# Turning the attention's value rows by VectorE blocks and a DRAM round trip in place of TensorE transposes

## The chip, the core and the metric

The kernel runs on one core of one Trainium2 chip. The metric is the device time of one execution in microseconds (us), as the median of several runs; lower is better. Engines are named as in the profile: PE is TensorE's matmul, PEld its weight load, DVE is VectorE, ACT is ScalarE, POOL is GpSimd, SP is SyncE, which here only issues DMAs. A name with q (SPq, DVEq) is an engine's instruction queue.

## What is computed

One step of a hybrid decoder layer: a prompt of 512 tokens and 8 samples of 4 tokens, model width 1024. The part that matters here is the sliding-window attention of the prompt:

```python
h = RMSNorm_pre(x)
x_r, q, k, v, g = split(h @ W_in)            # q: 8 heads of 128, k and v: 2 heads of 128
# per block of 128 queries: keys and values of this block and of the one before
s = q @ k.T * 128**-0.5 + rel_bias           # masked to the band
p = softmax(s with a learned sink per head)
o = p @ v                                    # (128 queries) x (128 columns of the head)
p_win_v = v[-128:]                           # the last 128 value rows are also an output
```

Beside it run an RG-LRU branch, an attention of the samples against a cache, gated output projections, and a convolutional feed-forward part.

## The kernel before

Activations are held turned, as columns by tokens: a projection tile is 128 columns (on partitions) by 512 prompt tokens and 32 sample tokens. Every float32 product is made of three fp32r matmuls: an operand X is split into a rounded part XH (ScalarE copy, L283, L710) and the rest XL (VectorE subtract, L168, L290), and the product is XH·WH, XL·WH and XH·WL, all by `mm` (L165).

The program is written as a list of *steps*. One step is one 128-column group of `W_in` on one half of the tokens (24 matmuls into a tile `pmin`), and behind each step stands a *tick*. A tick runs side jobs that are Python generators: each `yield` ends the job's turn, and `yield 3` skips two ticks. The order in which side jobs place their instructions between the steps is so the order on PE, DVE, ACT and POOL, which keep program order there. SP's order is made by the framework's scheduler. An engine works strictly in order, so an instruction that waits holds up all behind it.

The steps of this stage follow the list `qkv_order`: key 0, value 0, query heads 0 to 3, key 1, value 1, query heads 4 to 7. Side jobs between them:

- `attn_unit(hp, n)`, 16 of them: scores of two heads for query block n (tile `psc`, 6 matmuls), scaling and bias (`s`, DVE L177), softmax with exponentials on ACT (L781) and small DVE steps around them (`st`), a block transpose on DVE (`pb`, L823), its store to DRAM (`pd`, L826) and four loads back (`pt`, L831), the split of `pt` into `tH` (ACT, L834) and `tL` (DVE), and the product with the values (tile `pvp`: vH·tH, vL·tH, vH·tL). So the probabilities already go the way that the change gives to the values.
- `v_tok(kv, v)`, once for each of the two value heads: it turns the value tile `v` (head columns by tokens) to tokens by columns, which `pvp` needs as weights, splits it into `vH` and `vL`, and writes the last 128 rows to the output through `vout`.
- `sample_attn(g)`: the attention of the samples; its softmax ends at the DVE line L789 on tile `ss`, and PE turns the result at L911 (`pst`).
- weight splits (`wh_in`, `wl_in`) and weight loads (`raw_in`, 512 KB each, on SP), two weights ahead of their use.

Temporary tiles such as `v`, `s`, `tH` and `tL` come from one pool of 10 buffers (`T`), auxiliary PSUM tiles such as `pv`, `psc` and `pvp` from a pool of 5 (`PX`).

Of the kernel before, what the change touches and what calls it, by code (L numbers as in the profile page):

```python
# [11 lines left out]
F32 = mybir.dt.float32  # L12
F32R = mybir.dt.float32r
AF = mybir.ActivationFunctionType
# [3 lines left out]
P = 128  # L18
# [105 lines left out]
def hawk_step(ctx, tc, I, O):  # L124
    nc = tc.nc
    act, dve, pool, pe = nc.scalar, nc.vector, nc.gpsimd, nc.tensor
# [9 lines left out]
    drp = ctx.enter_context(tc.tile_pool(name="scratch", bufs=1, space=bass.MemoryType.DRAM))  # L136
# [9 lines left out]
    def T(name, dt=F32):  # L146
        return tp.tile([P, FLAT + 4], dt, tag="t", name=name)
# [7 lines left out]
    def PX(name):  # L155
        return psx.tile([P, 512], F32, tag="aux", name=name)

    def SM(name, shape, tag="sm"):
        return smp.tile(shape, F32, tag=tag, name=name)

    def f32(ap):
        return ap.bitcast(F32)
# [4 lines left out]
    def sub(out, a, b):  # L167
        dve.tensor_tensor(out=out, in0=a, in1=b, op=ALU.subtract)  # L168
# [51 lines left out]
    ident = keep.tile([P, P], F32, name="ident")  # L220
# [181 lines left out]
    pv = keep.tile([P, 96], F32, name="pv")  # L402
# [303 lines left out]
    Q, K, V, A = Full("q"), Full("k"), Full("v"), Full("a")  # L706
# [39 lines left out]
    vtmp = {}  # L746

    def v_tok(kv, v):
        px = PX(f"pv{kv}")
        for n in range(4):  # L750
            pe.transpose(px[:, n * P:(n + 1) * P], v[:, n * P:(n + 1) * P], ident)
        yield
        vh, vl = V.alloc(kv)
        act.activation(vh[:, 0:512], px, AF.Copy)
        sub(vl[:, 0:512], px, f32(vh[:, 0:512]))
        vo = SM(f"vout{kv}", [P, P])
        dve.tensor_copy(vo, px[:, 384:512])
        pool.dma_start(out=O["p_win_v"][0, 0, :, kv, :], in_=vo)
        yield

    def v_done(kv, a, ps):
        lo, hi = HALF[a]
        if a == 0:
            vtmp[kv] = T(f"v{kv}")
        v = vtmp[kv]
        scaled(v[:, lo:hi], ps, a)
        if a == 1:
            act.copy(vn[:, kv, :], v[:, SEQ:NT])
            start_at(now[0] + 1, v_tok(kv, v))
# [1030 lines left out]
    for i, x in enumerate(plan):  # L1800
# [8 lines left out]
        else:  # L1809
            _, q, c, a = x  # L1810
# [198 lines left out]
    v, r, s_, b_, h_ = (st[:, z:z + 1] for z in range(5))  # L2009
# [52 lines left out]
```

## Time and profile before

| what | value |
|---|---|
| median of 3 runs | 972.03 us (971.7 to 972.34) |
| the profiled execution | 972.46 us |
| its span, first to last instruction | 970.7 us |
| PE busy | 960.7 us, 99% |
| DVE busy | 761.6 us, 78% |
| ACT busy | 550.5 us, 57% |
| POOL busy | 167.9 us, 17% |
| mean granted TensorE clock | 0.999 of full speed (2.4 GHz) |
| DMA | 152 GB/s mean over the span |

All times of day below are in us from the start of the span. The profiled execution lasted 1.76 us longer than its span, and 0.43 us longer than the median run. A busy share is a mean over stages; what a change in one stage is worth is read from that stage's waits.

### The profile page before, as it was taken

Reading aid. Unit: us, or ns where it says so; the run is one execution under the profiler, and the core shown is the slowest. Engines: PE = TensorE matmul, PEld = TensorE weight load, DVE = VectorE, ACT = ScalarE, POOL = GpSimd, SP = SyncE. Lnnn points to the kernel's source line nnn. Section 1 sums busy time; section 2 is a strip of 40 time slices with the busy share of each in tenths; the row PEclk is TensorE's granted clock in tenths of the full one; section 3 lists DMA queues with packets and bytes.
Section 4 is the critical chain, followed back from the end, with each engine's and each line's share of the span. In section 5 each row is a group of like instructions: output and inputs, shape, how many; then the busy total and the mean of one; then the engine's idle time right before and its main releaser. Section 6 shows DMA issues by size and latency. Waiting matters only on the chain.

```text
span 970.7 us, 20070 instructions
## 1 busy us (share of the span) xinstructions
PE 960.7 (99%) x7598; PEld 952.3 (98%) x7598; DVE 761.6 (78%) x1623; ACT 550.5 (57%) x1342; POOL 167.9 (17%) x282
## 2 busy tenths in 40 slices
PE   9999999999999999999999999999999999999997
PEld 8999999999999999999999999999999999999996
DVE  5778888857858555599967878787888888888886
ACT  6544533467476425566867665555555565656642
POOL 2152000003406231230011110101011111111024
PEclk9999999999999999999999999999999999999999
DMA  7865435532334537236147576767667675858632
GB/s 222 239 216 182 146 92 146 154 106 88 96 99 152 177 107 187 64 106 195 46 108 196 133 182 147 183 153 175 162 160 189 151 192 136 205 132 232 185 136 92
DMA packets 248412, 147.26 MB, mean 152 GB/s; under 512 B 37332, under 2 KB 232796, under 8 KB 248284
## 3 DMA queue, kind: packets, MB, share of 16 engines
q1 hardware_dynamic: 237324, 124.15, 43.4%
q0 software_dynamic: 9696, 19.42, 11.7%
q10 hardware_dynamic: 1296, 2.43, 0.7%
q8 instruction: 59, 0.97, 0.4%
q14 instruction: 37, 0.30, 0.1%
HBM read 118.21 MB, written 16.74 MB: 139 GB/s over the span
## 4 chain that ended last, share of the span: by engine, by line
PE 89%; DVE 6%; ACT 2%; issue 1%; DMA 1%; POOL 0%; DVEq 0%; ACTq 0%; SPq 0%; POOLq 0%
PE pmin L165 20%; PE pux L1529 16%; PE pmdn L165 16%; PE puy L1529 8%; PE pq L1529 6%; PE pmlo L165 5%; PE pmao L165 5%; PE pmout L165 4%; PE puz L1529 4%; PE pg L165 1%; PE pvp L165 1%; PE psc L165 1%; DVE ft L174 0%; DVE wl_e L168 0%; DVE wl_dl L168 0%
## 5 line engine op out<-in xcount | busy, mean ns | idle before, releaser
L165 PE MATMUL pmin<-hH,wh_in 128*128 128x256 f32 (+1 forms) x568 | 163.9, 291 | 0.0
L165 PE MATMUL pmin<-hL,wh_in 128*128 128x256 f32 (+1 forms) x568 | 162.4, 288 | 0.0
L165 PE MATMUL pmin<-hH,wl_in 128*128 128x256 f32 (+1 forms) x568 | 159.1, 288 | 0.0
L165 PE MATMUL pmdn<-fH,wh_dn 128*128 128x256 f32 (+1 forms) x448 | 129.2, 288 | 0.0
L165 PE MATMUL pmdn<-fH,wl_dn 128*128 128x256 f32 (+1 forms) x448 | 129.0, 288 | 0.0
L165 PE MATMUL pmdn<-fL,wh_dn 128*128 128x256 f32 (+1 forms) x448 | 128.9, 288 | 0.0
L165 PEld LDWEIGHTS pmin<-hH,wh_in 128*128 128x128 f32 x568 | 107.2, 189 | 1.2 <-issue 1.0
L165 PEld LDWEIGHTS pmin<-hL,wh_in 128*128 128x128 f32 x568 | 107.2, 189 | 0.1
L165 PEld LDWEIGHTS pmin<-hH,wl_in 128*128 128x128 f32 x568 | 104.7, 188 | 0.2 <-issue 0.2
L177 DVE SCALAR_TENSOR_TENSOR uc<-u,fv,uc 128x560 f32<-128x560 f32 x128 | 102.0, 797 | 1.7 <-ACT uc L1560 1.1
L165 PEld LDWEIGHTS pmdn<-fH,wl_dn 128*128 128x128 f32 x448 | 84.4, 188 | 0.0
L165 PEld LDWEIGHTS pmdn<-fL,wh_dn 128*128 128x128 f32 x448 | 84.3, 188 | 0.1
L165 PEld LDWEIGHTS pmdn<-fH,wh_dn 128*128 128x128 f32 x448 | 84.3, 188 | 0.1
L1657 ACT COPY u<-pux 128x272 f32<-128x272 f32 x52 | 20.1, 387 | 86.5 <-PE pux L1529 86.5
L168 DVE TENSOR_TENSOR u<-puy,u 128x240 f32<-128x240 f32 (+2 forms) x78 | 24.6, 344 | 47.8 <-PE puy L1529 30.7
L174 DVE TENSOR_TENSOR ft<-ft,pmdn 128x256 f32<-128x256 f32 (+1 forms) x104 | 45.1, 434 | 16.4 <-PE pmdn L165 16.4
L283 ACT ACTIVATE wh_in<-raw_in 128x512 fp32r<-128x512 f32 x70 | 42.2, 625 | 19.0 <-issue 10.6
L290 DVE TENSOR_TENSOR wl_in<-raw_in,wh_in 128x512 fp32r<-128x512 f32 x70 | 47.8, 693 | 1.0 <-ACT wh_in L283 1.0
L1560 ACT ACTIVATE uc<-u,fv 128x560 f32<-128x560 f32 x64 | 48.2, 755 | 0.0
L781 ACT ACTIVATE s<-s,st 128x256 f32<-128x256 f32 (+1 forms) x32 | 15.2, 475 | 53.0 <-DVE st L778 45.3
L168 DVE TENSOR_TENSOR wl_dn<-raw_dn,wh_dn 128x512 fp32r<-128x512 f32 x56 | 38.3, 684 | 3.6 <-ACT wh_dn L1478 3.6
L1467 POOL DMA_DIRECT2D raw_up_s<-raw_up_s x26 | 22.4, 862 | 93.5 <-DMA raw_up_s<-raw_up__11280 5.4
(744 smaller groups left out, 3371.1 us busy)
## 6 DMA issues: line engine op xcount, KB each, us to landing
raw_in<-in_w_in_dram SPq DMA_DIRECT2D x35, 512.0 KB
raw_dn<-in_w_down_dram SPq DMA_DIRECT2D x56, 256.0 KB
raw_up_s<-in_w_up_dram SPq DMA_DIRECT2D x25, 512.0 KB
raw_up_s<-raw_up_s POOLq DMA_DIRECT2D x26, 256.0 KB, 4.2
raw_ao<-in_w_attn_o_dram SPq DMA_DIRECT2D x8, 512.0 KB
raw_lo<-in_w_lru_o_dram SPq DMA_DIRECT2D x8, 512.0 KB
raw_out<-in_w_out_dram SPq DMA_DIRECT2D x8, 512.0 KB
pd<-pb SPq DMA_DIRECT2D x12, 256.0 KB
```

The lines of the kernel that those rows point to most:

```text
L165: pe.matmul(out, l, r, start=start, stop=stop)
L168: dve.tensor_tensor(out=out, in0=a, in1=b, op=ALU.subtract)
L174: dve.tensor_tensor(out=out, in0=a, in1=b, op=ALU.add)
L177: dve.scalar_tensor_tensor(out=out, in0=a, scalar=s_, in1=b, op0=op0, op1=op1)
L283: act.activation(hl[0], raw, AF.Copy)
L290: (eng or dve).tensor_tensor(out=hl[1], in0=raw, in1=f32(hl[0]), op=ALU.subtract)
L781: act.activation(s3[:, j, :], s3[:, j, :], AF.Exp, bias=ng[:, j:j + 1], accum_out=sm[:, j:j + 1])
L1467: pool.dma_start(out=w["p4"], in_=w["p2"], accum_op=ALU.add)
L1529: pe.matmul(ps[:, :HN], w, x, start=start and k == 0 and i == 0, stop=stop and k == 3 and i == 2, skip_group_check=True)
L1560: act.activation(yt[j][:, 0:FLATU], u[:, 0:FLATU], AF.Copy, scale=fv[:, j:j + 1])
L1657: act.copy(e[nm_], z)
```

## The change

`v_tok` no longer uses PE. DVE turns the 16 32x32 blocks of each 128x128 piece in one instruction (`vb`), SP stores the result to DRAM (`vrows`), four SP loads bring it back with the blocks in their new places, into the tile `v` itself, and the split into `vH` and `vL` reads `v` in SBUF where it read PSUM. The copy for the output goes from DVE to ACT. The job now has three turns behind the first: the loads one tick later, the split three ticks after these, the output copy one tick after that.

```diff
     def v_tok(kv, v):
-        px = PX(f"pv{kv}")
-        for n in range(4):
-            pe.transpose(px[:, n * P:(n + 1) * P], v[:, n * P:(n + 1) * P], ident)
-        yield
-        vh, vl = V.alloc(kv)
-        act.activation(vh[:, 0:512], px, AF.Copy)
-        sub(vl[:, 0:512], px, f32(vh[:, 0:512]))
+        vb = T(f"vb{kv}")[:, 0:512]
+        dve.transpose(vb.rearrange("p (b n d) -> p n b d", b=4, n=4),
+                      v[:, 0:512].rearrange("p (n b q) -> p n b q", n=4, b=4))
+        rows = drp.tile([P, 512], F32, name=f"vrows{kv}")
+        nc.sync.dma_start(out=rows, in_=vb)
+        yield
+        src = rows.rearrange("(a q) (b x) -> b q a x", a=4, b=4)
+        for b in range(4):
+            nc.sync.dma_start(out=v[32 * b:32 * b + 32, 0:512].rearrange("p (a x) -> p a x", a=4), in_=src[b])
+        yield 3
+        vh, vl = (x[:, 0:512].rearrange("p (n a d) -> p n a d", n=4, a=4) for x in V.alloc(kv))
+        vt = v[:, 0:512].rearrange("p (a n d) -> p n a d", a=4, n=4)
+        act.activation(vh, vt, AF.Copy)
+        sub(vl, vt, f32(vh))
+        yield
         vo = SM(f"vout{kv}", [P, P])
-        dve.tensor_copy(vo, px[:, 384:512])
+        act.copy(vo.rearrange("p (a d) -> p a d", a=4), vt[:, 3])
         pool.dma_start(out=O["p_win_v"][0, 0, :, kv, :], in_=vo)
         yield
```

Lines behind this one move by 8 (L823 becomes L831, and so on). On PE the two groups of four transposes are gone and nothing else moves. On the other engines only the rows of `v_tok` move, and a few DMAs of SP beside them.

On SP this stands before, behind the loads of the weights for query heads 6 and 7 (`ohs` and `mk` are tables of the sample attention, `st_b` holds the recurrent states, `pd_0` and `pt_0` belong to attention unit 0):

```order
L259 DMA raw_in_1183<-in_w_in_dram 128x8x128
L669 DMA ohs<-in_c_ohs_dram 128x320
L826 DMA pd_0_831<-pb_0_829 128x256
L673 DMA mk_894<-in_c_msk_dram 128x320
L831 DMA pt_0_898<-pd_0_831 32x4x64 x4
L602 DMA st_b<-strow 32x8x32 x2
L826 DMA pd_1_973<-pb_1_971 128x512
```

And this stands there now:

```order
L753 DMA vrows_743<-vb_741 128x512
L259 DMA raw_in_1186<-in_w_in_dram 128x8x128
L757 DMA v_407<-vrows_743 32x4x128 x4
L834 DMA pd_0_827<-pb_0_825 128x256
L669 DMA ohs<-in_c_ohs_dram 128x320
L673 DMA mk_890<-in_c_msk_dram 128x320
L839 DMA pt_0_894<-pd_0_827 32x4x64 x4
L834 DMA pd_1_969<-pb_1_967 128x512
```

The store of value head 0 now stands ahead of a weight load and its four loads ahead of unit 0's store and the sample tables.

On DVE this stands before, between the softmax of attention unit 2 (`st_2`) and the key of head 1 (`ks_0`, `kL`):

```order
L168 TENSOR_TENSOR st_2_977<-sinkb,st_2_977 128x2
L290 TENSOR_TENSOR wl_in_942<-raw_in_668,wh_in_941 128x512
L171 TENSOR_TENSOR ks_0_1014<-pmin_0_914,rep 128x256
L174 TENSOR_TENSOR st_2_977<-st_2_977 128x2
L787 RECIPROCAL st_2_977<-st_2_977 128x2
L789 TENSOR_SCALAR s_2_975<-s_2_975,st_2_977 128x256 x2
```

And this now:

```order
L168 TENSOR_TENSOR st_2_973<-sinkb,st_2_973 128x2
L168 TENSOR_TENSOR vL_982<-v_407,vH_981 128x512
L290 TENSOR_TENSOR wl_in_938<-raw_in_668,wh_in_937 128x512
L171 TENSOR_TENSOR ks_0_1014<-pmin_0_910,rep 128x256
L174 TENSOR_TENSOR st_2_973<-st_2_973 128x2
L795 RECIPROCAL st_2_973<-st_2_973 128x2
```

`vL` of value head 0, which stood some 20 rows earlier, is now the first row behind the small softmax steps, ahead of the two rows that DVE did while ACT made the exponentials.

On ACT this stands before at the same place (`tH_0` is the split of unit 0's probabilities):

```order
L782 ACTIVATE st_2_977<-st_2_977 128x2
L283 ACTIVATE wh_in_1011<-raw_in_668 128x512
L710 ACTIVATE kH_1016<-ks_0_1014 128x256
L283 ACTIVATE wh_in_1071<-raw_in_714 128x512
L834 ACTIVATE tH_0_1083<-pt_0_898 128x256
```

And this now:

```order
L790 ACTIVATE st_2_973<-st_2_973 128x2
L761 ACTIVATE vH_981<-v_407 128x512
L283 ACTIVATE wh_in_1011<-raw_in_668 128x512
L765 COPY vout_1041<-v_407 128x128
L710 ACTIVATE kH_1016<-ks_0_1014 128x256
L283 ACTIVATE wh_in_1074<-raw_in_714 128x512
L842 ACTIVATE tH_0_1086<-pt_0_894 128x256
```

`vH` now stands behind the exponentials of unit 2, and `vout` is a row of ACT. For value head 1 the same rows stand later: `vb` behind the copy `kout` of key 1, `vL` behind unit 2 of the second head pair, `vout` behind the exponentials of its unit 3.

## Rows read from the trace of the kernel before

**Rows 1.** The page's part 1: busy us (share of the span) xinstructions, by engine.

```profile
PE 960.7 (99%) x7598; PEld 952.3 (98%) x7598; DVE 761.6 (78%) x1623; ACT 550.5 (57%) x1342; POOL 167.9 (17%) x282
```

**Rows 2.** Waits of PE, whole span: who waited for whom, us, times, longest.

```profile
PE ps_warm L165 <- POOL ones L219: 1.0, 1, 1.0
...
PE pst L911 <- DVE ss L789: 0.7, 1, 0.7
```

**Rows 3.** Stages: us, then each engine's busy us (xinstructions), clock, DMA share, GB/s.

```profile
160.00:170.00 10.00, 9.32 (x76) 9.12 (x74) 9.28 (x27) 4.42 (x17) 0.00 (x0) 1.00 0.45 107
```

**Rows 4.** Timeline of PEld, first group of transposes: start, us, engine, line, op, tiles.

```profile
41.88 0.47 PEld L751 LDWEIGHTS pv<-ident,v 128*128 128x128 f32 x4
42.32 0.19 PEld L165 LDWEIGHTS pmin<-hH,wh_in 128*128 128x128 f32 x1
```

**Rows 5.** Timeline of DVE, 40 to 54 us; in brackets idle before, and releaser.

```profile
40.96 1.29 DVE L290 TENSOR_TENSOR wl_in<-raw_in,wh_in 128x512 fp32r<-128x512 f32 x2
43.72 0.46 DVE L168 TENSOR_TENSOR qL<-pmin,qH 128x288 fp32r<-128x288 f32 x1 [1.47 <-ACT qs L712]
...
45.65 0.68 DVE L168 TENSOR_TENSOR vL<-pv,vH 128x512 fp32r<-128x512 f32 x1
46.25 0.28 DVE L757 COPY vout<-pv 128x128 f32<-128x128 f32 x1
...
53.06 0.46 DVE L168 TENSOR_TENSOR qL<-pmin,qH 128x288 fp32r<-128x288 f32 x1 [0.91 <-ACT qs L712]
53.43 0.70 DVE L823 STREAM_TRANSPOSE pb<-s 128x512 f32<-128x512 f32 x1
```

**Rows 6.** Timeline of SP: stores of probabilities and the loads behind them.

```profile
54.16 0.35 SPq L826 DMA_DIRECT2D pd<-pb  x1
...
56.23 2.02 SPq L831 DMA_DIRECT2D pt<-pd  x4
...
61.70 0.34 SPq L826 DMA_DIRECT2D pd<-pb  x1
68.22 1.77 SPq L831 DMA_DIRECT2D pt<-pd  x4
```

**Rows 7.** The chain that ended last, in order of time, 147 to 170 us.

```profile
147.87 4.37 DMA pt<-pd
...
168.87 0.40 DVE ss L789
...
169.41 0.30 PE pst L911
```

**Rows 8.** Timeline of ACT: end of unit 2's exponentials, and the second `vH`.

```profile
56.92 0.19 ACT L782 ACTIVATE st<-st 128x2 f32<-128x2 f32 x1
...
80.19 0.57 ACT L754 ACTIVATE vH<-pv 128x512 fp32r<-128x512 f32 x1
```

**Rows 9.** Timeline of DVE, 55 to 62 us.

```profile
55.87 0.68 DVE L290 TENSOR_TENSOR wl_in<-raw_in,wh_in 128x512 fp32r<-128x512 f32 x1
...
57.14 0.16 DVE L174 TENSOR_TENSOR st<-st 128x2 f32<-128x2 f32 x1 [0.26 <-ACT st L782]
...
59.30 0.46 DVE L171 TENSOR_TENSOR ks<-pmin,rep 128x288 f32<-128x288 f32 x1 [0.20 <-PE pmin L165]
```

**Rows 10.** Timeline of DVE at the second value head.

```profile
80.80 0.69 DVE L168 TENSOR_TENSOR vL<-pv,vH 128x512 fp32r<-128x512 f32 x1 [1.74 <-ACT vH L754]
...
81.61 0.68 DVE L290 TENSOR_TENSOR wl_in<-raw_in,wh_in 128x512 fp32r<-128x512 f32 x1
```

**Rows 11.** Timeline of DVE, 99 to 147 us.

```profile
99.86 0.68 DVE L168 TENSOR_TENSOR tL<-pt,tH 128x512 fp32r<-128x512 f32 x1
...
139.83 0.52 DVE L171 TENSOR_TENSOR xr<-pmin,rep 128x256 f32<-128x256 f32 x2 [0.19 <-PE pmin L165]
...
146.57 0.46 DVE L171 TENSOR_TENSOR ga<-pmin,rep 128x288 f32<-128x288 f32 x1 [1.85 <-PE pmin L165]
```

**Rows 12.** Timeline of PE: the first `tL` product of unit 1, second head pair.

```profile
103.79 0.28 PE L165 MATMUL pvp<-tL,vH 128*128 128x256 f32 x1
```

## The prediction

> **What bounds the kernel now.** I read the page's part 1 first: PE is busy for 960.7 of the 970.7 us of the span [rows 1], so what PE no longer does should come off the end. Then the waits of PE: five groups in the whole span, none above 1.0 us [rows 2]. One of them matters here. At the first turning of the sample attention's probabilities, PE waits 0.7 us for DVE (`pst` for `ss`). The stage view shows why: from 160 to 170 us DVE is busy 9.28 of 10 us while PE is at 9.32 [rows 3]. The chain that ended last says the same: ahead of `pst` at 169.41 it runs through DVE rows, not PE [rows 7]. So from the first key to that place two chains run side by side, PE's and the softmax's loop of DVE and ACT; at 169.4 us the loop ends last, by 0.7 us, and from there on PE leads again. Both must be followed.
>
> **What PE loses.** Two groups of four transposes go. From the first weight load of the first group to the load behind the group are 42.32 - 41.88 = 0.44 us [rows 4], 0.11 for each transpose; the second group, at 74.8, is alike. PE is never idle there, so without the eight it comes to 169 us earlier by 0.88 us, 0.09% of the time. The Trainium skill (VectorE: DVE Perf Modes, section The three transpose paths) gives 390 ns for a 128x128 transpose on TensorE in bf16; by that figure the eight would be 3.1 us, an estimate. The trace has the float32 ones here at 0.11 us, and that is used.
>
> **What DVE and ACT gain in work, value head 0.**
> - `vb`: one turning of 128x512. The same operation on the same shape (`pb`) takes 0.70 us; of `vL`, 0.68 long, the row behind it hides 0.08 [45.65 to 46.25, rows 5], so I take 0.6. It stands where two weight splits began at 40.96, and behind these DVE stood idle for 1.47 us [rows 5]: hidden. If that cover were gone it would be 0.6 us of DVE's loop.
> - The old `vL` and `vout` go from 45.65, some 0.6 + 0.2 us. This too is worth little: at 53.06 DVE waits again, for ACT's rounding of a product of PE [rows 5], so from there it is ahead by PE's 0.44 us and no more.
> - The new `vH` and `vL` stand behind unit 2's exponentials. These end at 56.92 + 0.19 = 57.11 [rows 8], 0.44 earlier now: 56.67. `vH` reads SBUF instead of PSUM; nearest is the old one, 0.57 [rows 8]. It ends at 57.15, since it begins some 0.1 before the row ahead ends. `vL` waits for it: before, DVE spent this time on a weight split and `ks` (55.87 to about 56.9) and so stood still for 0.26 only [rows 9]. Now these come behind `vL`: 57.15 + 0.6 + 0.6 + 0.4 = 58.75 for the row that stood at 57.14. That is 1.6 later; 0.2 to 0.3 is caught at once, since `ks` of the second half stood 0.20 waiting for PE [rows 9]. DVE's loop is late by 1.3 us.
> - `vout` on ACT: 0.2 us (of DVE's 0.28, rows 5, less overlap) ahead of a key split that waits for DVE anyway. Nothing.
>
> **Value head 1.** `vb` has no cover here and adds 0.6: 1.9 late. At 80.80 DVE waited 1.74 us for `vH`, and `vL` and `vout` then took until 81.61 [rows 10]. Gone from that place, they give back 0.8: 1.1 late. The new `vH` is hidden behind a rounding for which DVE waits first, `vL` adds 0.6: 1.7. `vout`, behind exponentials on ACT and ahead of a weight rounding, adds 0.2 to what DVE waits for next: 1.9 us late in absolute time at about 98 us, 1.9 + 0.88 = 2.8 us late against PE.
>
> **Where this lateness goes.** The idle stretches of DVE between 98 and 139 us end on ACT, which had itself waited for DVE; they move with the loop and absorb nothing. Two end on PE's product: 0.19 us at 139.83 and 1.85 us at 146.57 [rows 11]. They take 2.04 of the 2.8. DVE leaves 146.57 only 2.8 - 2.04 = 0.76 late against a PE that is 0.88 early: some 0.1 us earlier than before. From there to `pst` I read no other idle of DVE that PE ended, so `pst` starts at 169.41 - 0.1, and PE's wait there grows from 0.7 to about 1.5 us. Most of the gain is handed over to that wait.
>
> **Does PE wait anywhere before?** The nearest deadline is unit 1 of the second head pair: `tL` stood at 99.86 for 0.68 [rows 11], its product at 103.79 [rows 12]. With 1.9 more on DVE and 0.88 less on PE: 102.4 against 102.9, still 0.5 us of slack. A shortfall there would only be part of what `pst` waits for later.
>
> **SP and the round trip.** Ten DMAs are added, 1 MB in all. `vrows` 0 leaves SP at about 41.7, when `vb`, begun at 40.96, ends. The price of the trip: store to first load is 2.07 us (54.16 to 56.23) in the good case and 6.52 us (61.70 to 68.22) in the worst; four loads take 1.8 to 2.0 us to issue [rows 6]; landing 4.37 us in the longest case of the chain [rows 7]. The values are back between 41.7 + 2.1 + 2.0 + 4.4 = 50.2 and 54.7 us, and `vH` wants them at 56.6: hidden, with at least 1.9 us to spare. Behind the four loads wait unit 0's store and the sample tables, at worst until 50.2; unit 0's probabilities are then back at 50.2 + 2.1 + 2.0 + 4.4 = 58.7 us, about when ACT, done with the exponentials at 57.1 [rows 8] and with the rows behind them, comes to split them. For value head 1 the split stands some two units behind the store, and a unit takes 61.70 - 54.16 = 7.5 us [rows 6]. Weight loads moved by 2 to 3 us were issued two weights ahead. So SP costs nothing.
>
> **A rule that speaks against it.** The trip's loads read runs of 128 contiguous floats into 32 partitions, as `pt` does, and `pt` is back 4.4 us after issue [rows 7]. The Trainium skill (VectorE: DVE Perf Modes, section The three transpose paths) warns that a plain DMA which does the transpose by its strides is 19 times slower than the crossbar. By that the loads would take up to 19 x 4.37 = 83 us, the values would come near 129 us where 56.6 is wanted, and the kernel would take about 1044 us, an estimate. Here DVE does the turning inside blocks and the DMA only moves block rows, and the `pt` rows already show the price; I give this under 1 in 100.
>
> **Sum.** 972.46 - 0.1 = 972.35 us against the profiled execution. That one is 0.43 us above the median of the runs, so I forecast 971.9 us.
>
> **Rivals.**
> 1. *The gain is kept.* If `vL` finds its operand ready (ACT's order hides more than I read), or the loop catches up, DVE reaches 146.57 in time and all moves with PE: 972.03 - 0.88 = 971.2 us; with `pst`'s 0.7 us wait gone too, 970.5. For it: three of my steps on DVE are 0.6 us each and rest on overlap. Against it: DVE's busy share in this stage.
> 2. *Slower: the round trip is late.* `vL` stands on DVE ahead of all that follows. Each us by which the values land after 56.6 delays the loop by one, and past 57 the loop is the longer chain, so the end follows. To cost 0.2% (1.94 us) the values must land near 58.7, 17 us after the store, where the worst rows give 13. With both trips twice the worst (13.0 + 2.0 + 8.7 after 41.7) they land at 65.4: 8.8 us late, 971.9 + 8.8 = 980.7 us. For it: the store at 61.70 shows how slow one can be. Against it: its neighbour at 54.16, nearer in time, took a third of that [rows 6].
> 3. *The loop is later than I count.* Were `vb` of head 0 uncovered as well and the wait at 146.57 worth half, another 0.6 + 0.9: 973.4 us.
> 4. *The change frees nothing at all*, because PE's time in these rows is spent waiting behind weight loads: 972.0. PE shows no wait there, and this time is not told apart from the forecast.
>
> **How the numbers follow.** Two kernels that differ by less than 0.2% (1.9 us) can hardly be told from equal ones here. Chances: the forecast, with 0.5 us about it, 0.60; rival 1, 0.24; rival 3, 0.08; rival 2 and the rule, 0.06; rival 4 and others, 0.02. Range: down to rival 1's lower end with some spread of runs, 970.6; up to half way to rival 3 with that spread, 972.9. Faster by over 0.2% needs a gain above PE's 0.88 plus the whole 0.7 at `pst`: 0.04. Slower by over 0.2% is rival 2 and a tail of rival 3: 0.08. The same: 0.88.
>
> **What would show it.** In the changed profile: PE's two groups of transposes gone and PE's rows at 80 us earlier by about 0.9; DVE standing still some 1.6 us for `vH` at about 55.5; `tL` of unit 0 about 1.3 us later than before; the idle of 1.85 us at 146.57 nearly gone; PE's wait for `ss` at `pst` near 1.5 us; the four loads of `v` back before 55 us. I am wrong in the mechanism if `pst`'s wait stays at 0.7, and wrong in the sign if PE waits for `pvp` or for `wl_in` before 100 us.

## The result: slower by 1.36 us

The changed kernel takes 973.41 us (median of 22 runs, 972.62 to 974.26), the kernel before 972.05 us beside it (22 runs, 971.52 to 972.44). The ratio is 1.0014, 95% interval 1.0008 to 1.0020: less than the 0.2% that the prediction took to be hardly told from nothing, and with 22 runs each still clear of one. It is 1.5 us above the forecast and 0.5 us above the range's upper end. The profiled execution of the change took 972.82 us, so it is one of the quicker ones; a second profiled one, taken beside the experiments, took 973.19 us. Three single executions among all runs below took 1028.96, 1157.86 and 1331.01 us, at a granted clock of 0.85, 0.75 and 0.66 of full speed; they move no median by 0.1 us, and nothing is read from the trace of the one that has a trace.

The page's part 1 of the change (busy us, share, instructions) shows what was meant to happen: PE does eight matmuls less than in [rows 1], and 0.9 us less work.

```profile
PE 959.8 (99%) x7590; PEld 951.5 (98%) x7590; DVE 762.0 (78%) x1623; ACT 550.4 (57%) x1344; POOL 165.9 (17%) x282
```

The waits of PE in the change (who waited for whom, us, times, longest), beside [rows 2]:

```profile
PE pm_first L165 <- DVE wh_in L285: 1.1, 1, 1.1
...
PE pst L919 <- DVE ss L797: 0.7, 1, 0.7
PE pmin L165 <- DVE qL L168: 0.6, 1, 0.6
PE pq L1537 <- DVE b11L L168: 0.4, 1, 0.4
```

`pst` still waits 0.7 us, not 1.5. Two waits are new, one for `qL` at 99 us and one for `b11L` at 418 us. `pm_first`, in the start-up, moves between 0.3 and 1.1 us from execution to execution and has nothing to do with the change.

VectorE's timeline in the change (start, us, engine, line, operation, tiles; in brackets the idle time before it and what ended that):

```profile
40.34 0.71 DVE L750 STREAM_TRANSPOSE vb<-v 128x512 f32<-128x512 f32 x1
...
43.10 0.46 DVE L168 TENSOR_TENSOR qL<-pmin,qH 128x288 fp32r<-128x288 f32 x1 [0.87 <-ACT qs L712]
...
56.65 0.69 DVE L168 TENSOR_TENSOR vL<-v,vH 128x512 fp32r<-128x512 f32 x1 [1.72 <-ACT vH L761]
...
70.37 0.71 DVE L831 STREAM_TRANSPOSE pb<-s 128x512 f32<-128x512 f32 x1 [0.40 <-DMA pd<-pb]
...
75.79 0.70 DVE L750 STREAM_TRANSPOSE vb<-v 128x512 f32<-128x512 f32 x1
...
145.98 0.46 DVE L171 TENSOR_TENSOR ga<-pmin,rep 128x288 f32<-128x288 f32 x1 [0.30 <-PE pmin L165]
```

Much of this is as forecast. `vb` of value head 0 lies in front of an idle stretch (0.87 us are left of the 1.47 in [rows 5]). `vL` stands idle for `vH` for 1.72 us (forecast: some 1.6). The idle time ahead of `ga`, 1.85 us in [rows 11], is down to 0.30. The values are back in time: SP's timeline has their four loads issued from 43.78 on, and `vL` waits for ScalarE, not for a DMA.

```profile
41.08 0.35 SPq L753 DMA_DIRECT2D vrows<-vb  x1
...
43.78 1.77 SPq L757 DMA_DIRECT2D v<-vrows  x4
```

**Where the time went.** The second traces of both kernels start alike: the matmul of `pmin` at 33.93 us in before is at 33.96 us in the change. So they can be laid side by side. These rows are PE's and VectorE's timeline of before:

```profile
85.01 0.69 DVE L823 STREAM_TRANSPOSE pb<-s 128x512 f32<-128x512 f32 x1
...
97.23 0.42 DVE L168 TENSOR_TENSOR qL<-pmin,qH 128x256 fp32r<-128x256 f32 x1 [1.38 <-ACT qH L710]
...
99.96 0.30 PE L165 MATMUL pmin<-hH,wh_in 128*128 128x288 f32 x1
...
169.00 0.30 PE L911 MATMUL pst<-ident,ss 128*128 128x128 f32 x1 [0.67 <-DVE ss L789]
...
414.51 1.72 DVE L177 SCALAR_TENSOR_TENSOR h2f<-x,pvn,pst_f 128x272 f32<-128x272 f32 x4
...
522.07 0.30 PE L165 MATMUL pmdn<-fH,wh_dn 128*128 128x288 f32 x1
...
881.08 0.29 PE L1529 MATMUL puz<-b21H,wl_s_a 128*128 128x272 f32 x1
```

And the same rows of the change:

```profile
86.40 0.71 DVE L831 STREAM_TRANSPOSE pb<-s 128x512 f32<-128x512 f32 x1 [0.34 <-DMA pd<-pb]
...
99.49 0.42 DVE L168 TENSOR_TENSOR qL<-pmin,qH 128x256 fp32r<-128x256 f32 x1 [1.58 <-ACT qH L710]
...
99.97 0.40 PE L165 MATMUL pmin<-hH,wh_in 128*128 128x288 f32 x1 [0.74 <-DVE qL L168]
...
169.17 0.30 PE L919 MATMUL pst<-ident,ss 128*128 128x128 f32 x1 [0.66 <-DVE ss L797]
...
415.11 1.72 DVE L177 SCALAR_TENSOR_TENSOR h2f<-x,pvn,pst_f 128x272 f32<-128x272 f32 x4 [0.47 <-DVE pst_f L177]
...
522.67 0.29 PE L165 MATMUL pmdn<-fH,wh_dn 128*128 128x288 f32 x1
...
882.32 0.29 PE L1537 MATMUL puz<-b21H,wl_s_a 128*128 128x272 f32 x1
```

The distance between the same matmuls of the two traces, along the span:

| place | PE of the change against before | what happened since the place above |
|---|---|---|
| 34 us | +0.03 | |
| 90 us | -0.86 | eight transposes gone: -0.89 |
| 104 us | +0.13 | wait for `qL`: +0.99 |
| 169 us, at `pst` | +0.17 | +0.04 |
| 290 us | +0.25 | +0.08, in small pieces |
| 425 us | +0.59 | wait for `b11L`: +0.34 |
| 522 us | +0.60 | |
| 881 us | +1.24 | PE's pace, no wait in any row: +0.64 |
| 944 us | +1.28 | |

So the gain came, and three losses of 0.99, 0.34 and 0.64 us followed, in a stage where I looked at the wrong row and in two where I didn't look at all. Each is tested below.

### The profile page after: what moved, and what is told of

Same layout as the page of the kernel before. It is cut to its first block, busy times and chain, and to the rows that moved or that the text cites. A ratio compares the mean times of both kernels' runs of the same rounds, so it can differ in the third digit from the quotient of the medians.

```text
span 971.0 us, 20079 instructions
## 1 busy us (share of the span) xinstructions
PE 959.8 (99%) x7590; PEld 951.5 (98%) x7590; DVE 762.0 (78%) x1623; ACT 550.4 (57%) x1344; POOL 165.9 (17%) x282
## 4 chain that ended last, share of the span: by engine, by line
PE 84%; DVE 9%; ACT 3%; DMA 2%; issue 1%; SPq 0%; DVEq 0%; POOL 0%; ACTq 0%; POOLq 0%
PE pmin L165 16%; PE pux L1537 16%; PE pmdn L165 16%; PE puy L1537 8%; PE pq L1537 6%; PE pmlo L165 5%; PE pmao L165 5%; PE pmout L165 4%; PE puz L1537 4%; DMA pd<-pb 2%; PE pg L165 1%; PE pvp L165 1%; DVE wl_e L168 0%; DVE ft L174 0%; DVE st L784 0%
```

## The experiments

Times are medians of 11 runs (before once more: one run); the kernel before ran beside them at 972.08 us (first four), 972.07 (next four), 972.10 (next four) and 972.05 us (the rest). The letters of the theories are those of the expectations: A, the order and the work on VectorE and ScalarE make the softmax's loop late; B, the trip's own DMAs cost; C, the buffers of PSUM and of the pool `T` are dealt in another phase later. D to G and P came up on the way and are told where they first stand.

**The change again.**

> The changed kernel once more, for a second trace. Its median was 973.41 us, 1.36 above before, while its first trace, at 972.82, was one of its quicker runs. Theory A (order on DVE and ACT: vb, vL, vH and vout make the softmax loop late): PE has again a wait near 99 us for qL on DVE, longer than the 0.7 us of the first trace. Theory B (the trip's own DMAs delay the stores and loads of the probabilities): DVE's wait for a store to land near 70 us, 0.4 in the first trace, is longer. Theory C (other buffers later on: removing pv and adding vb shifts the rings of PSUM and temporary tiles): the first trace was 0.7 us longer than before between 437 and 944 us, spread over all matmuls, and 0.4 at 400 to 440; both must show again. Time 973.4.

Measured: 973.43 us (ratio 1.0015, 1.0006 to 1.0024). Its trace is the one laid against before above: both new waits and the lost 0.64 us come again, as A and C said. B's sign, a longer wait of `pb` near 70 us, does not come: `pb` waits 0.07 us there, and 0.34 us for another store at 86.40 instead.

**Before without the transposes, and nothing in their place.**

```diff
-        px = PX(f"pv{kv}")
-        for n in range(4):
-            pe.transpose(px[:, n * P:(n + 1) * P], v[:, n * P:(n + 1) * P], ident)
...
-        act.activation(vh[:, 0:512], px, AF.Copy)
+        act.activation(vh[:, 0:512], v[:, 0:512], AF.Copy)
```

> Before without the eight PE transposes and without anything in their place: the value rows are split unturned, at the old place, from SBUF. What the transposes are worth by themselves. A and B: 972.05 - 0.88 = 971.2 us, with PE's wait at pst unchanged at 0.7. C: the PSUM ring is shifted here as in the change, so if that is what costs, the time is 972.3 or more.

`vL` and `vout` read `v` unturned as well. Measured: 971.16 us, 0.92 less than before (ratio 0.9990, 0.9982 to 0.9999). The transposes are worth what the prediction gave for them, 0.88, and PE keeps it: in VectorE's timeline `qL` moves forward with PE, from 97.23 us to

```profile
96.83 0.42 DVE L168 TENSOR_TENSOR qL<-pmin,qH 128x256 fp32r<-128x256 f32 x1 [1.38 <-ACT qH L710]
```

and PE's wait at `pst` stays at 0.7 us, with all behind it 0.8 earlier. The loop follows PE where nothing makes it late. This kernel deals PSUM's buffers as the change does and shows no loss later, so C falls as far as it speaks of PSUM.

**The change without `vb` and without the trip.**

```diff
-        vb = T(f"vb{kv}")[:, 0:512]
-        dve.transpose(vb.rearrange("p (b n d) -> p n b d", b=4, n=4),
-                      v[:, 0:512].rearrange("p (n b q) -> p n b q", n=4, b=4))
-        rows = drp.tile([P, 512], F32, name=f"vrows{kv}")
-        nc.sync.dma_start(out=rows, in_=vb)
...
-        for b in range(4):
-            nc.sync.dma_start(out=v[32 * b:32 * b + 32, 0:512].rearrange("p (a x) -> p a x", a=4), in_=src[b])
```

> The change without vb and without the DRAM trip: the values stay unturned, and only the split stands at its new, later place, with vout on ACT. A: vH and vL behind unit 2's exponentials are 1.3 us of the 1.9 that I counted, so most of the loss is here: 972.2 to 972.8 us, with a wait of PE before 100 us or a longer one at pst. B: 971.2, as without the transposes alone. C: as e_noturn.

**The change with `vb`, without its ten DMAs.**

> The change with vb but without its DRAM trip: vb is made and not used, the values stay unturned. Only the ten DMAs are missing against the change. A: 973.2 to 973.4 us, as the change, with PE's wait near 99 us. B: at most 0.6 us above e_late (vb's own time), and 1 us or more below the change.

Measured: 972.48 us for the first of these two, 1.32 above the kernel without transposes; 972.95 us for the second, 0.47 more, where A wanted 973.2 or more and B 972.4 or less. The full change is another 0.48 above that. By medians, then, A has 1.79 of the 2.27 us that the change loses after its gain, and B 0.48. The traces cut it otherwise. With `vb` and no trip, PE waits 0.79 us for `qL` as in the change, and not for `b11L`. Without `vb`, `qL` starts at 98.40 and PE loses 0.3 us there. In both, `pb` waits for a store near 70 us (0.37 and 0.55), so that wait needs no trip. Both lose 0.64 to 0.73 us between 522 and 881 us, where no instruction of the change runs. So three things had to be separated: the wait for `qL` (A), the stall ahead of `b11L`, which only kernels with the trip had (E), and the slower pace of PE (D: work that the change moved makes it; D1: the copies `vout` on ScalarE do; D2: something else does).

**`vL` on GpSimd.**

```diff
-        sub(vl, vt, f32(vh))
+        pool.tensor_tensor(out=vl, in0=vt, in1=f32(vh), op=ALU.subtract)
```

> The change, with vL (the values' low part, twice 128x512) computed by GpSimd in place of VectorE; nothing left out. A (the lateness of VectorE and ScalarE decides): vL is 0.6 us of VectorE's late work each time, and VectorE no longer stands waiting for vH; by 99 us qL comes 1.2 us or more earlier than in the change (99.5), PE's wait for it (0.7 to 0.8 us) is gone, and the time is that of the change less 0.7 to 0.9: 972.6. GpSimd's own subtraction of this shape takes 1.29 us in the profile of before (wl_in) and nobody should wait for it. B (the trip's DMAs decide): 973.4, qL wait unchanged. D (what costs is a slower pace of PE between 520 and 880 us, 0.65 us in the traces of the change against before, together with 0.36 at 418 us): these stay in the trace whatever qL does; if they go too, 971.6.

Measured: 971.16 us (971.06 to 971.59), 2.27 below the change and 0.91 below before. Its highest run is below the lowest of the 33 of before (971.64), though the interval of the ratio, 0.9983 to 1.0001, just reaches one. Two of the three losses are gone from the trace, and 0.14 of the 0.64 us in the third are left. VectorE's and PE's timeline:

```profile
97.96 0.42 DVE L168 TENSOR_TENSOR qL<-pmin,qH 128x256 fp32r<-128x256 f32 x1 [1.58 <-ACT qH L710]
...
98.99 0.30 PE L165 MATMUL pmin<-hH,wh_in 128*128 128x288 f32 x1
...
521.18 0.29 PE L165 MATMUL pmdn<-fH,wh_dn 128*128 128x288 f32 x1
...
880.34 0.28 PE L1537 MATMUL puz<-b21H,wl_s_a 128*128 128x272 f32 x1
```

`qL` stands 1.5 us earlier than in the change and PE doesn't wait for it. GpSimd takes 1.31 us for `vL` where VectorE takes 0.69, and nobody waits for that. A's share is as expected; that the stall went and most of the slower pace with it A can't explain.

**`vout` back on VectorE.**

```diff
-        act.copy(vo.rearrange("p (a d) -> p a d", a=4), vt[:, 3])
+        dve.tensor_copy(vo.rearrange("p (a d) -> p a d", a=4), vt[:, 3])
```

> The change, with vout copied by VectorE as before instead of ScalarE; nothing left out. A: on ScalarE the copy stands right before the rounding and qH for which qL waits at 99 us (0.2 us); on VectorE it costs 0.2 us at another place of the same loop: 973.3 to 973.5, PE's wait for qL 0.6 to 0.8 us. D1 (the slower pace of PE between 520 and 880 us comes from the copies on ScalarE, two instructions more on its stream): the pace is that of before, 0.65 us less, 972.8. D2 (the pace has another cause): unchanged in the trace.

**Before with `vout` on ScalarE, nothing else.**

> The kernel before, with vout copied by ScalarE instead of VectorE and nothing else; nothing left out. A: 0.2 us less on VectorE, 0.28 on ScalarE where it is not late: 972.0, as before. D1 (the copies on ScalarE alone bring the slower pace of PE between 520 and 880 us): 972.7, and in the trace PE loses 0.65 us in that stretch against before. D2: no loss there.

Measured: 972.56 us and 972.20 us. In the first, `qL` starts at 98.78, 0.7 us earlier than in the change, and PE's wait for it is no longer listed. Two things make the 0.7. The idle time ahead of `qL` is 1.25 us where it was 1.58 (and 1.38 in before), so the copy's place on ScalarE has its 0.2 us; and `pb`, which waits 0.34 us for a store at 86.40 in the change, doesn't wait here, which A had not reckoned with. It also has no stall ahead of `b11L`. Its pace between 522 and 881 us is that of the change (359.65 us for the two matmuls that the table below uses). By D1 it would be that of before, so D1 falls. The second kernel is 0.13 above before (ratio 1.0003, 0.9994 to 1.0012), where D1 wanted 0.65; by itself that interval could not exclude it.

**Before, with `vb` and the trip beside its transposes.**

```diff
+        vb = T(f"vb{kv}")[:, 0:512]
+        dve.transpose(vb.rearrange("p (b n d) -> p n b d", b=4, n=4),
+                      v[:, 0:512].rearrange("p (n b q) -> p n b q", n=4, b=4))
+        rows = drp.tile([P, 512], F32, name=f"vrows{kv}")
+        nc.sync.dma_start(out=rows, in_=vb)
...
+        for b in range(4):
+            nc.sync.dma_start(out=v[32 * b:32 * b + 32, 0:512].rearrange("p (a x) -> p a x", a=4), in_=src[b])
```

> The kernel before, with its transposes on PE kept and used, and with vb and the ten DMAs of the round trip added beside them (the loads overwrite v, which nobody reads any more). Nothing of the output is changed. A: vb adds 0.6 us to VectorE at value head 1, well inside the 2.2 us that qL has in hand at 99 us in before: 972.1, no wait for qL. B (the ten DMAs cost 0.5 us wherever they stand): 972.5. E (the 0.5 us is the stall of VectorE ahead of h2f at 415 us, which only kernels with the trip showed): 972.4, and the trace shows PE's wait for b11L of 0.4 us at 418 us.

Measured: 972.24 us, 0.17 above before. There is no wait for `qL`. The stall of VectorE ahead of `h2f` and PE's wait for `b11L` (0.43 us) are there as E said, and PE keeps its quick pace, 359.06 us between the same two matmuls. So where the loop isn't late the ten DMAs cost nothing that a median shows but this stall, and B as I put it, a cost of the transfers wherever they stand, falls.

Next I looked at what the quick and the slow kernels have in common in the FFN. Their instructions there are the same, in the same order. The operands of its products come from the pool of SBUF slots (`S`), whose buffers are handed out as they come free; the values of head 1 take two of these slots, and the change takes them later. In the built programs `b11H`, `b11L` and the `fL` tiles of the FFN lay in one set of slots in every kernel with the slow pace that had run so far and in others in every quick one. That is theory F. It can be tried with no work moved:

**One more slot taken for a while, in before (F against D).**

```diff
+    def pad_buffer():
+        t = S("pad")
+        pool.memset(t[:, 0:1], 0.0)
+        yield 4
+        pool.memset(t[:, 1:2], 0.0)
+        yield
+
+    start_at(22, pad_buffer())
```

> The kernel before with one buffer more taken from the pool of slots (S, where the operands of PE live) for four steps of the schedule at 22, and GpSimd writing one column of it twice; nothing else, nothing left out. No work is moved; but the slots that later tiles get are dealt in another order, and in the FFN b11H, b11L and the fL tiles then lie in the slots in which they lie in the change. F (the slower pace of PE between 520 and 880 us comes from where the FFN's operands lie): PE loses 0.65 us in that stretch against before, time 972.7. D (the pace hangs on the work that the change moved): no loss, 972.05. A says nothing on it.

**The same at step 60, where it leaves the FFN's slots as they are (the control).**

> The kernel before with the slot taken for four steps at 60 instead of 22, and the same two writes of one column by GpSimd; nothing left out. At that step the taking changes no slot of the FFN's operands: they lie as in before. F (the pace hangs on where the operands lie): 972.1, no loss between 520 and 880 us. G (the two writes, or the mere presence of two more instructions, slow PE there): 972.7.

**The same at step 22, in the change.**

> The change with the same slot taken for four steps at 22 and nothing else, nothing left out. b11H, b11L and the fL tiles of the FFN then lie where they lie in the variant with vL on GpSimd, which kept the quick pace. F: PE's wait for qL at 99 us stays (0.75), the 0.65 us between 520 and 880 us are gone, 972.8. D: the pace stays that of the change, 973.4.

**The same at step 22, in the variant with `vL` on GpSimd.**

> The change with vL on GpSimd, and the slot taken for four steps at 22; nothing left out. One b11H of the FFN then lies where it lies in the change and in the slowed version of before, b11L and the fL tiles lie in a third way. F: the time rises from 971.16, by 0.3 to 0.65 if that b11H decides, by less or nothing if the others do; qL at 99 us stays unwaited for. D (only work moved early makes the pace): 971.2.

**Before once more, for its trace.**

> The kernel before once more, for a second trace. If the quick pace between 520 and 880 us belongs to the kernel, PE's rows there keep their distance from the first trace of before within 0.1 us; if it belongs to the execution, they part by 0.3 or more.

Measured: 972.72 us with the slot taken at 22, 0.62 above before (ratio 1.0007, 0.9998 to 1.0016); its lowest run is 972.61, and one of the 33 runs of before, at 972.70, lies above that. It is 0.21 us late already at 522 us, lost in small pieces. The control takes 972.02 us, as before. PE's timeline of the first:

```profile
522.24 0.30 PE L165 MATMUL pmdn<-fH,wh_dn 128*128 128x288 f32 x1
...
881.84 0.28 PE L1537 MATMUL puz<-b21H,wl_s_a 128*128 128x272 f32 x1
```

and of the control:

```profile
522.03 0.30 PE L165 MATMUL pmdn<-fH,wh_dn 128*128 128x288 f32 x1
...
881.05 0.29 PE L1537 MATMUL puz<-b21H,wl_s_a 128*128 128x272 f32 x1
```

The table has the time between these two matmuls, the same in all kernels. In no kernel does PE show a wait between them.

| kernel | from the one row to the other | median of the times |
|---|---|---|
| before, both traces | 359.01 and 359.01 | 972.05 |
| before, slot taken at 60 | 359.02 | 972.02 |
| before, slot taken at 22 | 359.60 | 972.72 |
| change, both traces | 359.65 and 359.65 | 973.43 |
| change, slot taken at 22 | 359.37 | 972.52 |
| `vL` on GpSimd | 359.16 | 971.16 |
| `vL` on GpSimd, slot taken at 22 | 359.65 | 971.59 |

F holds: with the same instructions in the same order, PE is 0.5 to 0.6 us slower or not over this stretch, according to the slots alone. The pace belongs to the kernel, since two traces of one kernel agree to 0.01 us, and two further writes by GpSimd don't make it. G falls, and D as the only cause. In the change itself the other slots gave back 0.28 us of the 0.64, where F wanted all of it, so that slots make the other 0.36 us there is not shown. The change with the slot taken also lost its stall ahead of `b11L`, so its 0.91 us are not the pace alone.

Which of the slots does it stays open, with one hint. The last variant was to rise by 0.3 to 0.65 us if the one `b11H` decides, since of the tiles named only that one lies in it as in the slowed kernels; it rose by 0.43, and by 0.49 in the stretch. But no run moved this tile alone, the change with the slot taken has it elsewhere and still takes 359.37, and the slowed version of before loses most between 640 and 760 us, the change between 520 and 700.

**Two writes more on VectorE, in the change (E1 against E2).**

```diff
+        t = S("pad")
+        dve.memset(t[:, 0:1], 0.0)
+        yield 4
+        dve.memset(t[:, 1:2], 0.0)
...
+    start_at(60, pad_buffer())
```

> The change with two writes of one column by VectorE at step 60 of the schedule (into a slot taken for them; the slots of the FFN's operands stay those of the change); nothing left out. E1 (VectorE's stall of 0.35 us ahead of h2f at 415 us hangs on where that instruction stands in VectorE's stream of instructions, since it showed only in the kernels with one certain number of instructions ahead of it): the stall is gone, PE's wait for b11L of 0.4 us with it, 973.1. E2 (it comes from the trip's DMAs or the lateness): it stays, 973.4. The pace between 520 and 880 us is that of the change by F and D.

Measured: 973.04 us, 0.39 below the change. VectorE's timeline:

```profile
70.66 0.71 DVE L831 STREAM_TRANSPOSE pb<-s 128x512 f32<-128x512 f32 x1 [0.54 <-DMA pd<-pb]
...
86.97 0.71 DVE L831 STREAM_TRANSPOSE pb<-s 128x512 f32<-128x512 f32 x1 [0.54 <-DMA pd<-pb]
...
415.33 1.72 DVE L177 SCALAR_TENSOR_TENSOR h2f<-x,pvn,pst_f 128x272 f32<-128x272 f32 x4
```

The stall of 0.47 us ahead of `h2f` is gone, PE's wait for `b11L` with it: E1, it hangs on the instruction's place in VectorE's stream. The kernels that stall have the same number of VectorE instructions ahead of `h2f` in the built program, all others another number. What the engine does in these 0.47 us no row shows: the releaser named there, VectorE's own row ahead, is as early as ever. The rows at 70.66 and 86.97 show another thing: `pb` waits for the store of an older block to land (one of three buffers). In the two traces of before it doesn't. In the change it waits at 70 us in the first trace (0.40) and at 86 us in the second (0.34), and here at both, 0.67 us more in all than in the second trace; the wait for `qL` is 1.2 us in this execution where it was 0.74. That the times of the change scatter over 1.6 us where those of before scatter over 0.9 may come from this; it was not tested.

**`vb` of value head 1 done twice (A against P, the prediction's step that lateness goes on to `pst`).**

```diff
+        if kv == 1:
+            dve.transpose(vb.rearrange("p (b n d) -> p n b d", b=4, n=4),
+                          v[:, 0:512].rearrange("p (n b q) -> p n b q", n=4, b=4))
```

> The change with vb of value head 1 done twice over, one more turning of 128x512 by VectorE at 76 us (0.63 us of its loop); nothing left out. A (PE has 2.2 us in hand for qL at 99 us and the change has used up more than that): PE's wait for qL grows by 0.6, from 0.75 to 1.35, and the time by as much, 974.0; its wait at pst stays 0.7. P (the prediction's step: lateness of VectorE's loop is handed on to the wait at pst): the wait at pst grows, the one for qL does not. B: no change, 973.4.

Measured: 974.25 us, 0.82 above the change. The waits of PE:

```profile
PE pmin L165 <- DVE qL L168: 1.2, 1, 1.2
...
PE pst L922 <- DVE ss L800: 0.7, 1, 0.7
PE pq L1540 <- DVE b11L L168: 0.4, 1, 0.4
```

VectorE's timeline has a second difference:

```profile
70.92 0.71 DVE L834 STREAM_TRANSPOSE pb<-s 128x512 f32<-128x512 f32 x1 [0.81 <-DMA pd<-pb]
```

So this trace mixes two causes. Against the second trace of the change, with starts alike, the longer wait of `pb` is 0.73 us, the second turning another 0.74, and at 86 us `pb` no longer waits: in all `qL` is 1.05 us later at 99 us. PE loses nearly all of that at matmuls that need a buffer which a `qL` has just emptied: 0.22 us at 84.6, 0.34 at 92.0 and 0.44 at the third, where 0.74 became 1.2. Nothing falls on `pst`, where PE still waits 0.7 us. P is refuted, and A's deadline holds. That the turning itself costs its 0.63 us rests on the medians alone, which grew by a little more, 0.82.

## Why the prediction was wrong

Two steps of the prediction failed: one sets the size of the miss, the other had the mechanism wrong.

**The term put at nothing: "from there on PE leads again".** The prediction's sum ends at `pst`. It has no term for what comes behind, and its only ground is that PE leads there. The row of `pst` measures this: it stands at 169.00 us in before and at 169.17 in the change, 0.14 late with starts alike, where the forecast had it 0.1 us early. That is 0.24 us of the 1.46 us between the forecast difference of -0.1 and the measured +1.36. With no more than that the change would have taken some 972.2 us, inside the range. Another 1.11 us arose behind `pst`: 0.34 in VectorE's stall and the wait for `b11L`, 0.64 in PE's pace, 0.13 in small pieces. The last 0.1 us lies between these two traces and the medians.

**The path: "Does PE wait anywhere before?"** The prediction looked at one deadline, `tL` of unit 1 in the second head pair, found 0.5 us of slack and stopped. A nearer one stands some three us ahead of it: a step of PE writes into a PSUM buffer that `qL` must have emptied. In the second trace of before, `qL` starts at 97.23 us and the matmul that needs its buffer at 99.96. In the change that matmul follows `qL`'s start by 0.48 us (99.49 to 99.97), so before had 99.96 - 97.23 - 0.48 = 2.25 us in hand. The prediction had itself worked out a lateness of 2.8 us against PE at just this time: 0.55 us over. The row stood in the trace and the sum was made; they were not laid together.

The prediction said that a shortfall there would be part of what `pst` waits for later. It isn't: once PE has stood still at 99 us, the loop is 2.25 us late against it, and the idle time of VectorE up to 147 us takes that; some 0.3 us of the 1.85 in [rows 11] are even left over. `pst` waits 0.7 us as before, in the change and, within 0.1 us, in every variant whose trace is read. That was the prediction's own sign of a wrong mechanism. The gain was handed over at `qL`, with a little more on top, and not at `pst`.

**Point by point.**
- PE loses 0.88 us: right, 0.92 by the kernel without transposes.
- `vb` of head 0 hidden: right. `vL` of head 0 idle for 1.6 us: right, 1.72.
- The loop late by 1.9 us at 98 us: 0.34 too little. With starts alike the second trace has it late by 1.36 us at 60 us (forecast 1.3), 2.09 behind `vb` of head 1 (1.9), 0.94 where the old `vL` and `vout` stood (1.1) and 2.24 at `qL`. What the forecast lacks is the wait of `pb` for a store at 86.40, 0.34 us; the first trace has 0.40 at 70.37 in its place. `vout` on ScalarE, sized at 0.2 us, has 0.20 (the idle time ahead of `qL` grew from 1.38 to 1.58).
- What that costs at `qL`: as the rows stand it is 99.49 - 97.23 = 2.26 us late, and PE is 0.88 early: 3.14, less the 2.25 in hand, is 0.89 us of PE's time lost, and PE's matmul there does stand 0.89 us behind where its lead of 0.88 would have put it.
- The two idle stretches absorb 2.0 us: they had that much to give, but no more than 1.75 was called on (1.85 became 0.30, the other is gone), the rest went into smaller gaps.
- SP and the trip cost nothing: right for the values, which are back in time; the trip beside the kept transposes adds 0.17 us. Not right for the stores of the probabilities, for which `pb` now waits 0.3 to 0.4 us. The wait at 70 us comes without a trip too; the one at 86 us shows only in two traces of kernels with the trip, and its cause was not tested. The rule that the prediction weighed against it (the Trainium skill, VectorE: DVE Perf Modes, section The three transpose paths, the plain DMA that is 19 times slower) did nothing here: `vL` waited for ScalarE alone. Its estimate took 19 times a load of `pt`, while the 19 of the Trainium skill is against the crossbar's transpose, which no row here has.
- Not looked at: everything behind `pst`. The prediction took the FFN to be unchanged. Its instructions are, and still the change lost 0.34 us there to a stall of VectorE and 0.64 us to PE's pace.

Rival 3 gave 973.4 us, which is what was measured, but by luck: `vb` of head 0 is covered, and the wait at 146.57 us took all that reached it. Rival 1's mechanism is real, as the kernel without transposes shows: a loop that isn't late moves with PE. The condition that I gave for a wrong sign, PE waiting for `pvp` or `wl_in` before 100 us, named the wrong tiles at the right time.

The sum as it came out: -0.89 for the transposes, +0.99 at `qL`, +0.12 in small pieces up to 290 us, +0.34 at `b11L`, +0.64 in pace, +0.05 in the rest: 1.25 us from 34 us on, against 1.36 between the medians.

**A better version** is the change with `vL` on GpSimd, 971.16 us, well below the change and 0.91 below before, with an interval that just reaches one. It keeps the gain of the transposes. Part of that is where its slots happen to fall: with a slot taken at step 22 it takes 971.59 us.

## What to carry to other kernels

When work moves from the bounding engine to one that feeds it, list every row in which the bounding engine takes over something from that engine, PSUM buffers that must be emptied among them, write the time in hand behind each, and compare the lateness with the smallest. A second engine that is idle there can take the work at twice the price and still win (here 1.31 us on GpSimd for 0.69 on VectorE). Where a forecast ends at one place of the span, say what it assumes of the rest. And a change of some tenths of a microsecond can't be read from the median alone: lay two traces side by side along the span, since a difference may arise hundreds of microseconds behind the edit, and a buffer taken and given back can show whether it is the edit's work or only where its tiles lie.

## What the runs showed of the hardware

PE's pace in a stretch without any wait depends on where the operands lie: 359.01 us or 359.60 for the same matmuls (0.16%), by the slots alone. The Trainium skill (SBUF — State Buffer, section SBUF: two separate sides) says that on the engines' side only the port pair shared by VectorE and GpSimd causes contention, and that PE never waits on anyone. By that rule the slots would change nothing and the slowed version of before would take the 972.10 us of before; it took 972.72, and no row names a cause. VectorE's stall of 0.47 us ahead of one instruction, which comes and goes with the number of instructions ahead of it, is as repeatable (it stands in all four traces of kernels with that number, and in none of the others) and as little explained.
